# A gated linear recurrence on one Trainium2 core: the diagonal and the first two levels of a chunk as one visit over groups of four tokens

## The chip, the core and the metric

The kernel runs on one core of a Trainium2 chip. The metric is the device time of one execution in microseconds (us), the median of several runs. The engines named below are TensorE (PE; PEld is its weight load), VectorE (DVE), ScalarE (ACT), GpSimd (POOL) and SyncE (SP), which starts the DMAs.

## What is computed

A two-layer model over 1024 tokens and 1024 channels in float32: sliding-window attention and a squared-ReLU MLP, then the HGRN2 recurrence and a second MLP. Only the recurrence is touched. It has 8 heads with 128 key and 128 value channels, and the tokens stand in chunks of 64:

```python
q, f, i, g = jnp.split(h @ w_in, 4, axis=-1)
forget = lb + (1.0 - lb) * jax.nn.sigmoid(f)
k = 1.0 - forget
...
b = jnp.cumsum(lc, axis=2)                    # lc = log(forget), one chunk
o_inter = einsum('bhtd,bhde->bhte', qc * jnp.exp(b), state)
diff = b[:, :, :, None, :] - b[:, :, None, :, :]
decay = jnp.exp(jnp.where(causal, diff, -jnp.inf))
scores = einsum('bhtd,bhtsd,bhsd->bhts', qc, decay, kc)
o_intra = einsum('bhts,bhse->bhte', scores, vc)
...
```

Inside a chunk the score of query t and key s is a sum over the channels of q[t] k[s], times the product of the forget gates of the tokens s+1 to t.

## The kernel before

Channels lie on the partitions and tokens on the free axis, in two halves of 512 tokens (NH = 2). A head has, for each half, tiles of 128 x 512 for q, f (the forget gate), k, v and the output gate g.

**The recurrence of a head** (`recurrence`, lines 1141 to 1229) builds the scores of all 16 chunks without a logarithm or an exponential, by levels. A diagonal visit (lg = -1) multiplies k by q for every chunk (16 matmuls of 64 columns) and keeps the diagonal by a mask; then q is multiplied by f. Level lg = 0 to 5 joins neighbouring groups of H = 2^lg tokens: 16 matmuls of 32 columns give k against the q of the later group of every pair, a predicated copy with the level's mask puts them into the scores, and `double` (line 1231) multiplies q of the later group by the earlier group's product of gates, k of the earlier group by the later group's, and the products of the gates with each other. A last visit joins chunks in pairs (`cross`), and two more pieces, one for each half, make the states and the outputs. The matmuls of a visit are float32 with 64 weight columns, so the two chunks of a pair lie in the two column halves of the array (`rows`, line 1158). A visit takes one PSUM bank of pool q. Each matmul names all q and k tiles as inputs, so that a visit starts as a whole.

**The pieces around it.** `recurrence` is a generator with 10 pieces: the diagonal, six levels, the cross visit and two halves. `interleave` (line 1312) puts those of head e between the 14 pieces of `gates` of head e + 1, at 10 per 14. A piece of `gates` is one product of the projections (`product`, line 567: 12 matmuls of 128 x 512 with three products of high and low parts); `two` (line 1082) makes 7 of them with Strassen's seven products for a pair of the matrices q, g and then f, v. `strassen_weights` (line 573) loads four raw weights and makes four sums in tiles of pool m; `weight_split` writes the high and low parts into pools wh and wl, five tiles each.

**The order of the work.** Every operation is first recorded (`Schedule.add`, line 150) with its engine, a cost and its tiles; `order` (line 184) then plans the whole kernel as a list schedule. On each engine the ready operation with the lowest rank goes next; the rank is the place in the program, less a lead of 100 for weights and for what empties a bank of pool p. Tiles of a pool are handed out in program order as they come free (BUFS, line 41). The costs are the code's own: 70 + 1.04 n ns for a product or a predicated copy on VectorE, and a drain of 120 ns when TensorE changes between matmuls of the whole array and of column halves. What comes out is a fixed order for each engine; on the chip each engine works its queue in that order and waits by semaphores.

Pools m (7 tiles) and t (18) hold tiles of 512 float32 numbers per partition. m serves the weight sums, the totals and states of the recurrence, attention's scores with their sinks, and the scaled sums of the MLP. t serves nearly everything else that is short-lived.

Of the kernel before, what the change touches and what calls it, by code (L numbers as in the profile page):

```python
# [10 lines left out]
F32 = mybir.dt.float32  # L11
F32R = mybir.dt.float32r
I32 = mybir.dt.int32
AF = mybir.ActivationFunctionType
ALU = mybir.AluOpType
AX = mybir.AxisListType

P = 128
# [3 lines left out]
NH = 2  # L22
# [17 lines left out]
PI_DOWN = float(np.float32(3.1415925))  # L40
BUFS = {"a": 60, "t": 18, "m": 7, "sm": 8, "wr": 5, "wh": 5, "wl": 5, "p": 4, "q": 4}
CH = 64
# [236 lines left out]
class Net:  # L279
# [490 lines left out]
    def rope_tables(self):  # L770
        shape = (P, NBLK, ROT // 2)
        pos = self.const((P, NBLK), I32)
        self.dma(pos, self.io["pos"], 4 * P * NBLK)
        posf = self.const((P, NBLK))
        self.op("DVE", self.nc.vector.tensor_copy, [posf], [pos], 100, posf, pos)
        ang = self.const(shape)
        for j, f in enumerate(INV_FREQ):
            self.ts("DVE", ang[:, :, j], posf, f, None, ALU.mult, None, NBLK)
        self.trig = []
        for shift in (0.25, 0.0):  # L780
            turns, r = self.const(shape), self.const(shape)
            n = NBLK * ROT // 2
            self.ts("DVE", turns, ang, float(0.5 / np.pi), shift, ALU.mult, ALU.add, n)
            self.ts("DVE", turns, turns, MAGIC, MAGIC, ALU.add, ALU.subtract, n)
            self.stt(r, turns, -TWO_PI[0], ang, ALU.mult, ALU.add, n)
            self.stt(r, turns, -TWO_PI[1], r, ALU.mult, ALU.add, n)
            self.stt(r, turns, -TWO_PI[2], r, ALU.mult, ALU.add, n)
            if shift:
                self.ts("DVE", r, r, float(np.pi / 2), None, ALU.add, None, n)
            self.ts("DVE", r, r, PI_DOWN, -PI_DOWN, ALU.min, ALU.max, n)  # L790
            self.act(r, r, AF.Sin, n)
            self.trig.append(r)
# [233 lines left out]
    def hgrn_constants(self):  # L1026
# [23 lines left out]
        self.level_mask = []  # L1050
        for lg in range(LEVELS):
            mask, later = self.const((P, CH), I32), self.t(I32, (P, CH))
# [4 lines left out]
            self.tt("DVE", mask, mask, later, ALU.mult, CH)  # L1057
            self.level_mask.append(mask)

    def put_by(self, views):  # L1060
# [80 lines left out]
    def recurrence(self, e, gates, totals, out):  # L1141
# [4 lines left out]
        scores = self.t(F32, (P, NC, CH))  # L1146
        tots, tot = [self.t(tag="m") for _ in range(NH)], [g[1] for g in gates]
        at = 0
        for lg in range(-1, LEVELS):
            H = 1 << max(lg, 0)  # L1150
            n, width = (1, CH) if lg < 0 else (CH // (2 * H), CH // 2)
            part = self.psum("q")[:, : NC * width].rearrange("p (c t) -> p c t", c=NC)
            later = lambda z: z if lg < 0 else z.rearrange("p (n a h) -> p n a h", a=2, h=H)[:, :, 1]
            both = [z for q, f, k, g, v in gates for z in (q, k)]
            for hf, (q, f, k, g, v) in enumerate(gates):
                for c in range(BPH):
                    for b in range(2):
                        rows = slice(b * CH, b * CH + CH)
                        j = 2 * c + b
                        self.mm(part[rows, hf * BPH + c], chunk(k, j), later(chunk(q, j)), True, True, CH, 2.06, "columns", both)  # L1160
            if lg < 0:
                mask = self.diag.unsqueeze(1).to_broadcast([P, NC, CH])
                self.tt("DVE", scores, part, mask, ALU.mult)
                for q, f, k, g, v in gates:
                    self.tt("any", q, q, f, ALU.mult)
                yield
                continue
            mask = later(self.level_mask[lg]).unsqueeze(1).to_broadcast([P, NC, n, H])
            target = scores.rearrange("p c (n a h) -> p c n a h", a=2, h=H)[:, :, :, 1]
# [21 lines left out]
        for hf, (q, f, k, g, v) in enumerate(gates):  # L1191
# [36 lines left out]
            out[hf].append(self.put_by(y) if keep else y)  # L1228
            yield

    def double(self, H, gates, tot, tots, at):

# [164 lines left out]
```

## Time and profile before

| | before |
|---|---|
| median of 3 runs | 2162.72 us (2162.41 to 2163.83) |
| profiled execution, its own time | 2167.06 us |
| its span | 2165.3 us |
| granted TensorE clock, mean | 0.995 |
| TensorE matmul busy | 2130.3 us (98%), 11464 instructions |
| weight load busy | 1721.6 us (80%) |
| VectorE busy | 1801.3 us (83%), 3531 instructions |
| ScalarE busy | 855.2 us (39%) |
| GpSimd busy | 60.5 us (3%) |
| float32 matmuls of 64 weight columns and 32 columns (levels) | 1536 instructions, 54.0 us busy |
| the same with 64 columns (diagonal, cross) | 384 instructions, 18.6 us busy |
| predicated copies of the levels, VectorE | 48, 25.8 us busy |

The profile is that of one execution. Its span goes from the first to the last instruction; the execution's own time holds a little more. In its lines L333 is the line of the helper that records every operation, so the tiles tell operations apart: out<-in by pool name, then the weight size, the shapes and a count. A float32 matmul stands as two instructions. A matmul's end is modelled, so the distance from start to start says more than the duration. "idle before <-releaser" is time in which the engine waited, and for what.

### The profile page before, as it was taken

The numbers are of one execution on the slowest core, as the hardware profiler recorded it, in microseconds if no ns is written. First come the engines' busy times: TensorE is split into PE (matmuls) and PEld (weight loads), VectorE is DVE, ScalarE is ACT, GpSimd is POOL, SyncE is SP. The second block draws the span as 40 slices with busy tenths as digits, with TensorE's granted clock in tenths as the row PEclk, the third lists the DMA queues.
The fourth block names the chain that finished last, engine by engine and source line by source line (L and its number), as shares of the span: only waits on it lengthen the run. The fifth ranks groups of instructions, "written<-read, shape, count | busy, mean of one in ns | idle before, by whom it ended". The sixth has DMA issues, their size and how long they took to land.

```text
span 2165.3 us, 32388 instructions
## 1 busy us (share of the span) xinstructions
PE 2130.3 (98%) x11464; PEld 1721.6 (80%) x11464; DVE 1801.3 (83%) x3531; ACT 855.2 (39%) x1791; POOL 60.5 (3%) x121
## 2 busy tenths in 40 slices
PE   9999999999999999999999999999999999999998
PEld 7778777888887887877788888888788887888887
DVE  8889889666789888899888888878877678988886
ACT  5567764212234233365333333343421223423444
POOL 4020000000000000000100000000000000000000
PEclk9999999999999999999999999999999999999999
DMA  6212273333368867741111111547333336976652
GB/s 210 79 49 83 79 241 99 112 107 107 111 219 298 261 208 230 249 135 54 59 55 59 55 59 59 186 156 228 101 109 107 103 117 218 301 254 211 216 180 78
DMA packets 174274, 316.50 MB, mean 146 GB/s; under 512 B 19616, under 2 KB 21664, under 8 KB 174112
## 3 DMA queue, kind: packets, MB, share of 16 engines
q1 hardware_dynamic: 174112, 314.43, 45.1%
q8 instruction: 90, 1.47, 0.3%
q14 instruction: 72, 0.59, 0.1%
HBM read 250.39 MB, written 63.96 MB: 145 GB/s over the span
## 4 chain that ended last, share of the span: by engine, by line
PE 54%; issue 36%; DVE 5%; ACT 3%; DMA 2%; SPq 0%; POOL 0%; POOLq 0%; ACTq 0%; DVEq 0%
PE p L333 28%; PE q L333 26%; DVE a L333 2%; DVE t L333 1%; ACT a L333 1%; ACT t L333 1%; DVE wl L333 1%; DVE m L333 1%; DMA a<-d 1%; DMA wr<-in_down 0%; ACT wh L333 0%; DMA wr<-in_wqkv 0%; DMA a<-in_x 0%; DVE sm L333 0%; DVE wh L333 0%
## 5 line engine op out<-in xcount | busy, mean ns | idle before, releaser
L333 PE MATMUL q<-a,wh 128*128 128x512 f32 x2560 | 799.7, 395 | 8.7 <-DVE t L333 3.7
L333 PE MATMUL p<-a,wh 128*128 128x512 f32 x2336 | 752.7, 401 | 4.1 <-ACT wh L333 3.3
L333 PEld LDWEIGHTS q<-a,wh 128*128 128x128 f32 x2560 | 480.9, 188 | 123.1 <-ACT t L333 5.2
L333 PEld LDWEIGHTS p<-a,wh 128*128 128x128 f32 x2336 | 431.7, 189 | 100.1 <-ACT wh L333 4.2
L333 PE MATMUL q<-a,wl 128*128 128x512 f32 x1280 | 500.1, 394 | 0.2 <-DVE wl L333 0.2
L333 PE MATMUL p<-a,wl 128*128 128x512 f32 x1168 | 462.5, 397 | 1.8 <-DVE wl L333 1.7
L333 PEld LDWEIGHTS q<-a,wl 128*128 128x128 f32 x1280 | 240.8, 188 | 57.5 <-DVE wl L333 0.6
L333 PEld LDWEIGHTS p<-a,wl 128*128 128x128 f32 x1168 | 220.3, 189 | 51.9 <-DVE wl L333 2.7
L333 DVE TENSOR_TENSOR wl<-wr,wh 128x512 fp32r<-128x512 f32 x352 | 240.6, 685 | 15.2 <-ACT wh L333 6.2
L333 ACT COPY t<-q 128x512 f32<-128x512 f32 (+2 forms) x201 | 111.7, 562 | 356.8 <-PE q L333 348.6
L333 DVE TENSOR_TENSOR a<-t,a 128x512 fp32r<-128x512 f32 (+1 forms) x294 | 194.3, 682 | 2.3 <-DMA t<-d 2.0
L333 DVE TENSOR_TENSOR wl<-m,wh 128x512 fp32r<-128x512 f32 x256 | 176.0, 688 | 16.5 <-ACT wh L333 7.3
L333 ACT CAST wh<-m 128x512 fp32r<-128x512 f32 x155 | 96.6, 623 | 219.5 <-PE q L333 151.2
L333 DVE CAST wh<-wr 128x512 fp32r<-128x512 f32 x189 | 80.7, 427 | 117.3 <-PE p L333 71.7
L333 DVE TENSOR_TENSOR t<-t,t 128x512 f32<-128x512 f32 (+3 forms) x265 | 157.0, 610 | 18.3 <-DMA t<-d 13.4
L333 ACT CAST a<-t 128x512 fp32r<-128x512 f32 x195 | 118.2, 619 | 127.3 <-PE q L333 82.5
L333 ACT CAST wh<-wr 128x512 fp32r<-128x512 f32 x163 | 100.6, 620 | 167.5 <-PE p L333 100.3
L333 DVE TENSOR_TENSOR m<-wr,wr 128x512 f32<-128x512 f32 x160 | 109.4, 686 | 27.3 <-DMA wr<-in_up 12.9
L333 PE MATMUL p<-wh,a 128*128 128x512 f32 x384 | 126.3, 399 | 0.4 <-ACT a L333 0.2
L333 PEld LDWEIGHTS q<-t,t 128*64 128x64 f32 (+1 forms) x2160 | 98.0, 144 | 25.1 <-PE p L333 10.9
L333 PE MATMUL q<-t,t 128*64 128x32 f32 (+2 forms) x2160 | 111.5, 230 | 0.0
L333 DVE CAST wh<-m 128x512 fp32r<-128x512 f32 x101 | 43.4, 429 | 75.3 <-PE q L333 61.8
(118 smaller groups left out, 2113.1 us busy)
## 6 DMA issues: line engine op xcount, KB each, us to landing
t<-d SPq DMA_DIRECT2D x296, 256.0 KB, 4.7
wr<-in_down SPq DMA_DIRECT2D x256, 256.0 KB, 4.0
d<-t SPq DMA_DIRECT2D x180, 256.0 KB, 2.6
wr<-in_up SPq DMA_DIRECT2D x128, 256.0 KB, 3.0
wr<-in_win SPq DMA_DIRECT2D x68, 256.0 KB, 2.9
a<-d SPq DMA_DIRECT2D x60, 256.0 KB, 4.4
wr<-in_wqkv SPq DMA_DIRECT2D x48, 256.0 KB, 3.0
d<-a SPq DMA_DIRECT2D x48, 256.0 KB, 3.4
```

The lines of the kernel that those rows point to most:

```text
L333: fn(*[place(a) for a in args], **{k: place(v) for k, v in kw.items()})
```

## The change

The diagonal and the levels lg = 0 and 1 become one piece, `fours`, over groups of four tokens. Before the matmuls, VectorE makes for each half a tile w with six more columns of queries for each group of four (the queries of tokens 1, 2 and 3 multiplied by the gates that lie between them and the keys of the same group). 16 matmuls of 64 columns then give k against q, and 16 of 96 columns k against w; they take three banks of pool q. One masked product and six predicated copies put the results into the scores. Fourteen more products bring q, k and the totals to where `double` left them after lg = 1. The levels lg = 2 to 5 stay. `recurrence` has 8 pieces instead of 10; `interleave` is called with the same numbers.

Pool t goes from 18 tiles to 17 and pool m from 7 to 6; the angle and turn tables of the rotary embedding, three constants before, are taken from pool t. The masks of the first two levels go, and three masks for the groups of four come.

```diff
@@ -38,7 +38,7 @@
 MAGIC = 12582912.0
 TWO_PI = (6.28125, 2029.0 / 2**20, 2 * np.pi - 6.28125 - 2029.0 / 2**20)
 PI_DOWN = float(np.float32(3.1415925))
-BUFS = {"a": 60, "t": 18, "m": 7, "sm": 8, "wr": 5, "wh": 5, "wl": 5, "p": 4, "q": 4}
+BUFS = {"a": 60, "t": 17, "m": 6, "sm": 8, "wr": 5, "wh": 5, "wl": 5, "p": 4, "q": 4}
 CH = 64
 LEVELS = 6
 K_SPANS = ((-1, 3), (2, 6), (5, 8))
@@ -769,16 +769,17 @@
 
     def rope_tables(self):
         shape = (P, NBLK, ROT // 2)
+        flat = lambda: self.t()[:, : NBLK * ROT // 2].rearrange("p (n d) -> p n d", n=NBLK)
         pos = self.const((P, NBLK), I32)
         self.dma(pos, self.io["pos"], 4 * P * NBLK)
         posf = self.const((P, NBLK))
         self.op("DVE", self.nc.vector.tensor_copy, [posf], [pos], 100, posf, pos)
-        ang = self.const(shape)
+        ang = flat()
         for j, f in enumerate(INV_FREQ):
             self.ts("DVE", ang[:, :, j], posf, f, None, ALU.mult, None, NBLK)
         self.trig = []
         for shift in (0.25, 0.0):
-            turns, r = self.const(shape), self.const(shape)
+            turns, r = flat(), self.const(shape)
             n = NBLK * ROT // 2
             self.ts("DVE", turns, ang, float(0.5 / np.pi), shift, ALU.mult, ALU.add, n)
             self.ts("DVE", turns, turns, MAGIC, MAGIC, ALU.add, ALU.subtract, n)
@@ -1048,7 +1049,7 @@
         self.diag = self.const((P, CH))
         self.ts("DVE", self.diag, bits, 0, None, ALU.is_equal, None, CH)
         self.level_mask = []
-        for lg in range(LEVELS):
+        for lg in range(2, LEVELS):
             mask, later = self.const((P, CH), I32), self.t(I32, (P, CH))
             self.ts("DVE", mask, bits, lg, None, ALU.logical_shift_right, None, CH)
             self.ts("DVE", mask, mask, 1, None, ALU.is_equal, None, CH)
@@ -1056,6 +1057,17 @@
             self.ts("DVE", later, later, 0, None, ALU.is_gt, None, CH)
             self.tt("DVE", mask, mask, later, ALU.mult, CH)
             self.level_mask.append(mask)
+        same, s4, d4 = (self.t(I32, (P, CH)) for _ in range(3))
+        self.ts("DVE", same, bits, 2, None, ALU.logical_shift_right, None, CH)
+        self.ts("DVE", same, same, 0, None, ALU.is_equal, None, CH)
+        self.ts("DVE", s4, si, 3, None, ALU.bitwise_and, None, CH)
+        self.tt("DVE", d4, ti, si, ALU.subtract, CH)
+        self.four_mask = []
+        for z, value in ((s4, 0), (d4, 1), (s4, 1)):
+            mask = self.const((P, CH), I32)
+            self.ts("DVE", mask, z, value, None, ALU.is_equal, None, CH)
+            self.tt("DVE", mask, mask, same, ALU.mult, CH)
+            self.four_mask.append(mask)
 
     def put_by(self, views):
 
@@ -1144,13 +1156,13 @@
         NC = NH * BPH
         chunk = lambda z, j: z[:, j * CH : j * CH + CH]
         scores = self.t(F32, (P, NC, CH))
-        tots, tot = [self.t(tag="m") for _ in range(NH)], [g[1] for g in gates]
-        at = 0
-        for lg in range(-1, LEVELS):
-            H = 1 << max(lg, 0)
-            n, width = (1, CH) if lg < 0 else (CH // (2 * H), CH // 2)
+        tots = [self.t(tag="m") for _ in range(NH)]
+        at, tot = yield from self.fours(gates, scores, tots)
+        for lg in range(2, LEVELS):
+            H = 1 << lg
+            n, width = CH // (2 * H), CH // 2
             part = self.psum("q")[:, : NC * width].rearrange("p (c t) -> p c t", c=NC)
-            later = lambda z: z if lg < 0 else z.rearrange("p (n a h) -> p n a h", a=2, h=H)[:, :, 1]
+            later = lambda z: z.rearrange("p (n a h) -> p n a h", a=2, h=H)[:, :, 1]
             both = [z for q, f, k, g, v in gates for z in (q, k)]
             for hf, (q, f, k, g, v) in enumerate(gates):
                 for c in range(BPH):
@@ -1158,14 +1170,7 @@
                         rows = slice(b * CH, b * CH + CH)
                         j = 2 * c + b
                         self.mm(part[rows, hf * BPH + c], chunk(k, j), later(chunk(q, j)), True, True, CH, 2.06, "columns", both)
-            if lg < 0:
-                mask = self.diag.unsqueeze(1).to_broadcast([P, NC, CH])
-                self.tt("DVE", scores, part, mask, ALU.mult)
-                for q, f, k, g, v in gates:
-                    self.tt("any", q, q, f, ALU.mult)
-                yield
-                continue
-            mask = later(self.level_mask[lg]).unsqueeze(1).to_broadcast([P, NC, n, H])
+            mask = later(self.level_mask[lg - 2]).unsqueeze(1).to_broadcast([P, NC, n, H])
             target = scores.rearrange("p c (n a h) -> p c n a h", a=2, h=H)[:, :, :, 1]
             part = part.rearrange("p c (n h) -> p c n h", n=n)
             self.op("DVE", nc.vector.copy_predicated, [target], [mask, part], 70 + NC * width * 1.04, target, mask, part)
@@ -1228,6 +1233,63 @@
             out[hf].append(self.put_by(y) if keep else y)
             yield
 
+    def fours(self, gates, scores, tots):
+        nc, NC, W = self.nc, NH * BPH, 6 * CH // 4
+        chunk = lambda z, j: z[:, j * CH : j * CH + CH]
+        N, new, more = TH // 4, [], []
+        for hf, (q, f, k, g, v) in enumerate(gates):
+            w = self.tile("w", 2, (P, 6 * N), F32)
+            qv, fv = (z.rearrange("p (n b) -> p n b", b=4) for z in (q, f))
+            wv = w.rearrange("p (n c) -> p n c", c=6)
+            mul = lambda out, x, y, n: self.tt("DVE", out, x, y, ALU.mult, n * N)
+            mul(wv[:, :, 0:1], qv[:, :, 1:2], fv[:, :, 1:2], 1)
+            mul(wv[:, :, 1:4:2], qv[:, :, 2:4], fv[:, :, 2:4], 2)
+            mul(wv[:, :, 2:6:3], wv[:, :, 1:4:2], fv[:, :, 1:3], 2)
+            mul(wv[:, :, 4:5], wv[:, :, 5:6], fv[:, :, 1:2], 1)
+            more.append(w)
+        diag = self.psum("q").rearrange("p (c t) -> p c t", c=NC)
+        six = [self.psum("q")[:, : BPH * W].rearrange("p (c t) -> p c t", c=BPH) for _ in range(NH)]
+        both = [z for q, f, k, g, v in gates for z in (q, k)] + more
+        for hf, (q, f, k, g, v) in enumerate(gates):
+            for c in range(BPH):
+                for b in range(2):
+                    rows, j = slice(b * CH, b * CH + CH), 2 * c + b
+                    self.mm(diag[rows, hf * BPH + c], chunk(k, j), chunk(q, j), True, True, CH, 2.06, "columns", both)
+        for hf, (q, f, k, g, v) in enumerate(gates):
+            for c in range(BPH):
+                for b in range(2):
+                    rows, j = slice(b * CH, b * CH + CH), 2 * c + b
+                    self.mm(six[hf][rows, c], chunk(k, j), more[hf][:, j * W : j * W + W], True, True, W, 2.0, "columns", both)
+        self.tt("DVE", scores, diag, self.diag.unsqueeze(1).to_broadcast([P, NC, CH]), ALU.mult)
+        for hf in range(NH):
+            part = six[hf].rearrange("p c (n k) -> p c n k", k=6)
+            target = scores[:, hf * BPH : hf * BPH + BPH].rearrange("p c (n b) -> p c n b", b=4)
+            for mask, t, src, m in zip(self.four_mask, (1, 2, 3), (slice(0, 5, 2), slice(1, 4, 2), slice(5, 6)), (3, 2, 1)):
+                mask = mask.rearrange("p (n b) -> p n b", b=4)[:, :, t:].unsqueeze(1).to_broadcast([P, BPH, CH // 4, m])
+                out, in_ = target[:, :, :, t:], part[:, :, :, src]
+                self.op("DVE", nc.vector.copy_predicated, [out], [mask, in_], 70 + BPH * CH // 4 * m * 1.04, out, mask, in_)
+        for hf, (q, f, k, g, v) in enumerate(gates):
+            qv, fv, kv = (z.rearrange("p (n b) -> p n b", b=4) for z in (q, f, k))
+            wv = more[hf].rearrange("p (n c) -> p n c", c=6)
+            mul = lambda out, x, y, n: self.tt("DVE", out, x, y, ALU.mult, n * N)
+            first = fv[:, :, 0:1]
+            mul(qv[:, :, 0:1], qv[:, :, 0:1], first, 1)
+            mul(qv[:, :, 1:4], wv[:, :, 0:5:2], first.to_broadcast([P, N, 3]), 3)
+            mul(kv[:, :, 2:3], kv[:, :, 2:3], fv[:, :, 3:4], 1)
+            tail = self.t()[:, : 2 * N].rearrange("p (n b) -> p n b", b=2)
+            mul(tail[:, :, 1:2], fv[:, :, 2:3], fv[:, :, 3:4], 1)
+            mul(tail[:, :, 0:1], fv[:, :, 1:2], tail[:, :, 1:2], 1)
+            mul(kv[:, :, 0:2], kv[:, :, 0:2], tail, 2)
+            new.append(tots[hf][:, :N].only(4))
+            mul(new[hf].unsqueeze(2), first, tail[:, :, 0:1], 1)
+        yield
+        return N, new
     def double(self, H, gates, tot, tots, at):
 
         n, new = TH // (2 * H), []
```

## Prediction

> **What bounds the kernel now.** I read the busy time by stage first, then TensorE's waits inside the recurrence stage, then single visits in order of time. Columns of the first view: stretch, its length, busy time (and instructions) of TensorE matmul, weight load, VectorE, ScalarE, GpSimd, then granted clock, DMA share, GB/s.
>
> ```profile
> 85.00:292.00 207.00, 202.61 (x1191) 158.35 (x1190) 183.64 (x407) 148.88 (x480) 21.39 (x49) 1.00 0.28 85
> 292.00:1003.00 711.00, 701.86 (x3030) 565.86 (x3031) 585.72 (x1033) 258.01 (x455) 0.37 (x2) 1.00 0.55 177
> 1003.00:1440.00 437.00, 434.98 (x3692) 352.80 (x3691) 377.43 (x866) 155.86 (x327) 9.68 (x18) 1.00 0.24 77
> 1440.00:2166.00 726.00, 710.29 (x3195) 580.33 (x3194) 583.39 (x1023) 245.44 (x442) 3.87 (x3) 0.99 0.54 173
> ```
>
> The recurrence runs from 1003 to 1440 us. TensorE is idle there for 437.00 - 434.98 = 2.0 us in all; VectorE is busy 377.43 / 437 = 86%, ScalarE 36%. TensorE's matmul ends are modelled, so I also ask what it waits for in that stage:
>
> ```profile
> PE q L333 <- DVE m L333: 1.0, 2, 0.6
> PE q L333 <- ACT t L333: 0.7, 2, 0.4
> PE q L333 <- DVE a L333: 0.4, 1, 0.4
> ```
>
> Five waits, 2.1 us. So in this stage a microsecond taken off TensorE's queue is a microsecond off the end, and work on another engine costs nothing until TensorE has to wait for it. The place of the change, in the middle of one head (start, duration, operation, count):
>
> ```profile
> 1182.83 0.39 PE L333 MATMUL p<-a,wl 128*128 128x512 f32 x1
> 1183.15 1.15 PE L333 MATMUL q<-t,t 128*64 128x64 f32 x32
> 1184.23 0.74 PE L333 MATMUL p<-a,wh 128*128 128x512 f32 x2
> ...
> 1185.04 0.62 PE L333 MATMUL p<-a,wh 128*128 128x512 f32 x2
> ...
> 1185.74 0.63 PE L333 MATMUL p<-a,wh 128*128 128x512 f32 x2
> ...
> 1186.90 0.40 PE L333 MATMUL p<-a,wl 128*128 128x512 f32 x1
> 1187.22 1.12 PE L333 MATMUL q<-t,t 128*64 128x32 f32 x32
> 1188.28 0.72 PE L333 MATMUL p<-a,wh 128*128 128x512 f32 x2
> ```
>
> The projections (p<-a) of the next head run without a break; between them stand the visits (q<-t,t). Three projection matmuls take 1185.74 - 1185.04 = 0.70 us, 0.23 each. The diagonal visit (64 columns, 16 matmuls shown as 32 instructions) pushes the next projection from 1182.83 to 1184.23: 1.40 us, less the 0.23 that the matmul before it takes, is **1.17 us**. The first level's visit (32 columns) pushes from 1186.90 to 1188.28: 1.38 - 0.23 = **1.15 us**. Half the columns cost the same. The instructions come in pairs, one for each column half of the array. What one takes by itself:
>
> ```profile
> L333 PE MATMUL q<-t,t x2160: 222/223/377, 1017.4 to 1438.1; 128*64 128x32 f32 x140, 128*64 128x64 f32 x34, 128*128 128x128 f32 x23
> L333 PE MATMUL q<-t,a x368: 276/379/430, 85.9 to 290.7; 128*64 128x256 f32 x120, 128*128 128x256 f32 x64
> ```
>
> The last one's modelled 0.22 us (the median of the first row, in ns) aside, 16 pairs start within 1.12 - 0.22 = 0.90 us at 32 columns and 0.93 at 64: 0.06 us a pair, whatever the width. The rest of each visit, 1.17 - 0.93 = 0.24 us, is the change of form before and after.
>
> **What goes and what comes on TensorE.** Per head, a 64-column and two 32-column visits go: 1.17 + 1.15 + 1.15 = 3.47 us. A 64-column set and, behind it in the same form, a 96-column set come. No instruction of 96 columns is in the trace. One side is the 64-column row: 0.06 us a pair. The other is the 256-column row of attention, in the same form:
>
> ```profile
> 143.97 3.24 PE L333 MATMUL q<-t,a 128*64 128x256 f32 x28
> 147.14 0.33 PE L333 MATMUL q<-c,a 128*128 128x128 f32 x1
> ```
>
> 28 instructions are 14 pairs; one takes 0.38 (the row above), so 13 steps take 3.24 - 0.38 = 2.86 us, 0.22 a pair. Between 0.06 at 64 and 0.22 at 256 columns a straight line gives 0.06 + 0.16 x 32/192 = 0.087 us at 96. I take that, since the width governs at 256 and the 64-column set sits where it just begins to. Then 16 x 0.087 = 1.39 us, and the new visit costs 1.17 + 1.39 = 2.56 us. Saved: 3.47 - 2.56 = **0.91 us a head, 7.3 us over eight heads**. At 0.06 a pair it would be 16 x 0.06 = 0.96 us, saved 1.34 a head, 10.7 in all. Should the planner put projections between the two sets, one more change of form (0.24) comes back: 0.67 a head, 5.4 in all.
>
> A rule speaks against the line. The Trainium skill (TensorE: Matmul & The Clock Gate, Part 3, "The mechanism") says that a weight load overlaps matmuls in flight only where their row groups differ; here both halves use all 128 rows. By that rule load and stream would add up, which is the second rival below; the trace does not bear it out, since 256 columns at 0.22 us a pair leave no room for a load on top.
>
> **What comes on VectorE.** Steps between starts (shown durations overlap by about 0.08):
>
> ```profile
> 1143.60 0.43 DVE L333 COPY_PREDICATED t<-c,q 128x256 f32<-128x256 int32 x1
> 1143.93 1.42 DVE L333 TENSOR_TENSOR t<-t,m 128x256 f32<-128x256 f32 x4
> 1145.27 0.68 DVE L333 SCALAR_TENSOR_TENSOR t<-t,t 128x512 f32<-128x512 f32 x1
> ...
> 1185.43 1.29 DVE L333 TENSOR_TENSOR t<-t,t 128x512 f32<-128x512 f32 x2
> 1186.63 0.69 DVE L333 TENSOR_TENSOR m<-wr,m 128x512 f32<-128x512 f32 x1
> ...
> 1188.84 0.73 DVE L333 COPY_PREDICATED t<-c,q 128x256 f32<-128x256 int32 x1
> 1189.37 1.46 DVE L333 TENSOR_TENSOR t<-t,t 128x256 f32<-128x256 f32 x4
> 1191.13 0.43 DVE L333 CAST wh<-wr 128x512 fp32r<-128x512 f32 x1 [0.31 <-PE p L333]
> ```
>
> A product of 512 takes (1186.63 - 1185.43)/2 = 0.60 us, of 256 (1145.27 - 1143.93)/4 = 0.335; that is 0.07 + 0.00104 n, so 0.20 at 128 and 0.47 at 384. A predicated copy of 256 takes 0.53 at the first level (1188.84 to 1189.37) and 0.33 at the third (1143.60 to 1143.93): short runs are slow, 0.07 + 0.0018 n. The new copies have runs of one to three elements, so I take the slow price.
> - Before, a head: diagonal mask 0.60, q by f twice 0.60, first level 0.53 + 4 x 0.345 + two totals of 256 at 0.335, second level 0.53 + 4 x 0.345 + two totals of 128 at 0.20: 6.7 us in 17 instructions.
> - After: the six columns, (128 + 256 + 256 + 128) a half, 1.08, twice: 2.2; mask 0.60; copies of 192, 128 and 64 a half, 0.42 + 0.30 + 0.19, twice: 1.8 (fast price: 1.2); then five products of 128, one of 384, one of 256 a half, 1.82, twice: 3.6. Sum 8.2 us in 29 instructions.
>
> That is 1.5 us more a head, 12 us in all; VectorE goes from 377 of 437 us to about 389 of 430, 91%. TensorE hides it as long as the next visit is not late, which is the one new wait. From the new visit to the third level's visit VectorE has copies and 14 products to do, about 5.5 us instead of the 2 of a level. In-order TensorE meets that visit where the planner put it; what is queued behind it is the next head's projections, and everything on TensorE waits with them. The planner's costs in the code (70 + 1.04 n ns) give the six copies 1.22 us, I 1.8: a slip of 0.58. What a slip does is seen in the last head, where the visits come as soon as they can:
>
> ```profile
> 1410.09 1.47 DVE L333 TENSOR_TENSOR t<-t,t 128x256 f32<-128x256 f32 x4
> 1411.47 0.69 DVE L333 TENSOR_TENSOR wl<-wr,wh 128x512 fp32r<-128x512 f32 x1
> ```
> ```profile
> 1411.38 0.39 PE L333 MATMUL p<-a,wh 128*128 128x512 f32 x1
> 1411.70 1.12 PE L333 MATMUL q<-t,t 128*64 128x32 f32 x32
> ```
>
> There copy and products took 0.53 + 1.38 = 1.91 us against 1.68 planned, and the visit still followed its forerunner after 0.32 us, as at 1182.83 and 1186.90. A slip of 0.23 is swallowed; of 0.58 at most 0.35 shows, less what VectorE's own pauses (0.31 us at 1191.13) take up. I put **0.2 us a head, 1.6 us** on TensorE, with 0 and 0.35 as ends. The 2.2 us for the six columns delay the new visit, and projections fill the time.
>
> **Edits priced at nothing.** The setup keeps 30 mask operations of 64 columns. The rope tables keep theirs and only change buffers. The new visit holds three q banks instead of one; the products use p banks, and ScalarE, which empties the transposes' banks ahead, is idle 64% of the stage. The recurrence now has 8 pieces, still spread at 10 per 14 steps, so its last pieces and their stores to DRAM go through SP's queue earlier in each head; the DMA share is 0.24, and none of TensorE's five waits is for a DMA. Pool m goes from 7 to 6. In attention GpSimd writes the sinks ahead into every m tile that comes free:
>
> ```profile
> L333 ACT COPY m<-q x6: 348/370/375, 86.3 to 95.5; 128x256 f32<-128x256 f32 x6
> L333 PE MATMUL q<-c,m x4: 272/273/300, 95.4 to 95.8; 128*128 128x128 f32 x4
> L333 POOL TENSOR_SCALAR m<-c x1: 226/226/226, 96.2 to 96.2; 128x4 f32<-128x4 f32 x1
> ```
>
> When it refills the first freed tile (96.2) only three blocks (six copies) have begun, one of them ended: seven tiles were taken, three at work. Six are enough. For t, 18 to 17, no view counts the live tiles. TensorE's waits in the other stages are 4.4, 9.1 and 15.7 us (first view); a tenth of them, 3 us, bounds what a new order of the same work does there, either way. I take 0.
>
> **Sum.** The profiled execution took 2167.06 us, 1.8 more than its span and 4.3 more than the median of the three runs. 2167.06 - 7.3 + 1.6 = 2161.4; the same -5.7 from the median 2162.72 is **2157.0 us**. A measurement tells about 0.2% from no change, 4.3 us.
>
> **Rivals.**
> 1. *VectorE's longer chain shows in full (0.18).* If the slip of 0.58 and 0.15 more from strided products (14 of them, 0.01 each by the first level's 0.345 against 0.335) all land on TensorE at the third level's visit, 8 x 0.73 = 5.8 us come back: -7.3 + 5.8 gives 2161.2, no change. For it: VectorE at 91%. Against: TensorE's waits on VectorE in this stage are 1.4 us today.
> 2. *Loads add to the stream at 96 columns (0.06).* The 0.06 a pair at 32 columns would be a load floor, and a 96-column pair would take 0.06 + 0.087: 16 x 0.147 = 2.35 us instead of 1.39, 7.7 us more in all: -5.7 + 7.7 = +2.0, 2164.7. Against: the 256-column row, and 32 and 64 columns costing alike.
> 3. *Slower: the weights' sums run out of m tiles (0.09).* The rows:
>
> ```profile
> 1170.86 1.11 DVE L333 SCALAR_TENSOR_TENSOR m<-m,m,q 128x128 f32<-128x128 f32 x3 [0.91 <-ACT m L333]
> ...
> 1177.72 0.34 DVE L333 SCALAR_TENSOR_TENSOR m<-m,m,q 128x128 f32<-128x128 f32 x1
> 1177.98 0.68 DVE L333 TENSOR_TENSOR m<-wr,wr 128x512 f32<-128x512 f32 x1
> ...
> 1183.53 0.69 DVE L333 TENSOR_TENSOR wl<-m,wh 128x512 fp32r<-128x512 f32 x1
> ```
>
> Each set of projections sums its weights in four m tiles; two totals and up to two state tiles hold four more (1170.86 to 1177.98), and the next set's first sum does start right behind the last state. With six tiles it may start one tile's life, up to 7 us, later. Five weight buffers of one product (12 matmuls, 2.8 us) each are ahead, so it decides only once about 11 us are used up. Two microseconds beyond that in each head are 16 us: 2157.0 + 16 = 2173. Against: no wait on wl is among TensorE's five.
>
> The forecast has 0.60; 0.07 is left for an order of the other stages that gives or takes more than 3 us. **Range:** low 2151.5, the 0.06 price (-10.7) with no wait, 2152.0, and a little of the other stages; high 2164.7, the second rival. **Chances:** faster by over 0.2%: 0.61 (nearly all of the forecast and half the 0.07), the same: 0.28, slower: 0.11.
>
> **What would show it.** In the profile after: a 64- and a 96-column set back to back, the second some 1.4 us long (0.087 a pair), and six visits a head where there were eight; VectorE 12 us busier in the stage; the third level's visit following its projection after more than 0.32 us in most heads if the first rival holds; waits for wl if the third. I am wrong if the stage from the first to the last visit is not 4 to 9 us shorter, or if another stage moves by more than 3.

## The result, and the profile after

The kernel after took **2176.40 us** (median of 6 runs, 2174.40 to 2178.09), the kernel before beside it 2162.56 (6 runs, 2162.24 to 2165.05). The ratio is 1.0062, 95% interval 1.0049 to 1.0074: slower by 13.8 us, where 5.7 us less had been forecast. The profiled execution took 2177.95 us, span 2176.2.

The stages of the kernel after from 292 us on, in the columns of the first view of the prediction:

```profile
292.00:1003.00 711.00, 701.55 (x3023) 565.63 (x3024) 584.00 (x1028) 256.68 (x452) 0.36 (x2) 0.99 0.53 177
1003.00:1440.00 437.00, 426.21 (x3419) 346.58 (x3418) 388.56 (x927) 167.79 (x356) 8.17 (x18) 1.00 0.23 76
1440.00:2176.00 736.00, 718.10 (x3217) 586.07 (x3217) 586.43 (x1028) 248.18 (x447) 3.85 (x3) 0.99 0.52 171
```

In the recurrence VectorE is busy 11 us more, about the forecast 12. But TensorE, idle for 2.0 us there before, now has 437.00 - 426.21 = 10.8 us of idle time. What it waits for between 1010 and 1445 us (in total, times, longest):

```profile
PE q L333 <- DVE t L333: 6.0, 7, 1.1
PE q L333 <- ACT t L333: 4.3, 6, 0.8
PE q L333 <- DVE a L333: 0.4, 1, 0.4
```

Seven waits for VectorE and six for ScalarE: nearly one of each in every head. TensorE in order of time, in one head of the middle:

```profile
1184.40 0.66 PE L333 MATMUL q<-c,t 128*128 128x128 f32 x4 [0.71 <-ACT t L333]
...
1186.29 0.39 PE L333 MATMUL p<-a,wl 128*128 128x512 f32 x1
1186.61 1.15 PE L333 MATMUL q<-t,t 128*64 128x64 f32 x32
1187.59 1.49 PE L333 MATMUL q<-w,t 128*64 128x96 f32 x32
1189.01 0.73 PE L333 MATMUL p<-a,wh 128*128 128x512 f32 x2
...
1193.29 0.63 PE L333 MATMUL p<-a,wh 128*128 128x512 f32 x2
1193.84 0.66 PE L333 MATMUL q<-t,t 128*64 128x32 f32 x16
1195.27 0.66 PE L333 MATMUL q<-t,t 128*64 128x32 f32 x16 [0.77 <-DVE t L333]
1195.86 0.50 PE L333 MATMUL p<-a,wl 128*128 128x512 f32 x1
```

The new visit is as forecast: two sets back to back. They push the next projection from 1186.29 to 1189.01, 2.72 us. Less the 0.23 of the matmul before them that is **2.49 us** (forecast 2.56). TensorE stops twice in this head. The third level's visit falls into two halves of 16 instructions, and the second waits 0.77 us for VectorE. Earlier in the head the transposes at 1184.40 wait 0.71 us for ScalarE. What VectorE does ahead of each (start, duration, operation):

```profile
1179.14 0.41 DVE L333 TENSOR_TENSOR w<-t,t 128x128 f32<-128x128 f32 x1
1179.44 0.39 DVE L333 TENSOR_TENSOR t<-t 128x128 f32<-128x128 f32 x1
1179.74 0.51 DVE L333 TENSOR_TENSOR w<-t,t 128x256 f32<-128x256 f32 x1
1180.12 0.38 DVE L333 TENSOR_TENSOR t<-t,t 128x128 f32<-128x128 f32 x1
1180.41 0.50 DVE L333 TENSOR_TENSOR w<-w,t 128x256 f32<-128x256 f32 x1
...
1182.01 0.69 DVE L333 TENSOR_TENSOR t<-t,a 128x512 f32<-128x512 f32 x1
...
1190.15 0.45 DVE L333 COPY_PREDICATED t<-c,q 128x192 f32<-128x192 int32 x1
...
1194.21 0.67 DVE L333 TENSOR_TENSOR wl<-wr,wh 128x512 fp32r<-128x512 f32 x1
1194.81 0.41 DVE L333 TENSOR_TENSOR t<-t,t 128x256 f32<-128x256 f32 x1
```
```profile
1182.73 0.63 ACT L333 ACTIVATE t<-t 128x512 f32<-128x512 f32 x1 [2.35 <-DVE t L333]
```

From start to start a product of 128 elements takes 1179.44 - 1179.14 = 0.30 us. The plan's cost and the prediction's were 0.20. The row product at 1182.01, which ScalarE's step at 1182.73 is waiting for, stands behind five such products. The keys' last product (1194.81), which the third level's second half is waiting for, ends a row of six copies and eight products that begins at 1190.15.

Outside the recurrence the wait that stands out is just ahead of it, TensorE first, then VectorE:

```profile
975.25 1.18 PE L333 MATMUL p<-a,wh 128*128 128x512 f32 x4
982.48 0.79 PE L333 MATMUL p<-a,wl 128*128 128x512 f32 x1 [6.05 <-DVE wl L333]
```
```profile
976.92 2.50 DVE L333 TENSOR_TENSOR t<-t,t 128x512 f32<-128x512 f32 x4
979.33 0.69 DVE L333 TENSOR_TENSOR m<-wr,m 128x512 f32<-128x512 f32 x1
...
981.73 0.69 DVE L333 TENSOR_TENSOR wl<-m,wh 128x512 fp32r<-128x512 f32 x1
```

A weight sum (m<-wr,m) and the low half made from it (wl<-m,wh) stand in VectorE's order behind row products, and the projection waits 6.05 us. The granted clock is low for a while (the last three columns are granted clock, DMA share and GB/s):

```profile
976.00:982.40 6.40, 0.43 (x2) 0.00 (x0) 6.40 (x12) 6.40 (x13) 0.00 (x0) 0.76 0.16 41
982.40:989.30 6.90, 6.82 (x22) 5.46 (x23) 6.90 (x13) 1.40 (x4) 0.00 (x0) 0.72 0.11 38
```

The 6.90 us after the wait run at 0.72: 1.9 us lost on top of the 6.05. The kernel before has its own, shorter stop near there, 46 us earlier:

```profile
936.40 1.81 PE L333 MATMUL p<-a,wh 128*128 128x512 f32 x4 [3.11 <-ACT wh L333]
```
```profile
937.00:941.00 4.00, 4.00 (x12) 3.10 (x12) 4.00 (x12) 2.47 (x5) 0.00 (x0) 0.61 0.00 0
```

So there are two places to test: the recurrence, and the stages around it.

### The profile page after: what moved, and what is told of

Same layout as the page of the kernel before. It is cut to its first block, busy times and chain, and to the rows that moved or that the text cites. A ratio compares the mean times of both kernels' runs of the same rounds, so it can differ in the third digit from the quotient of the medians.

```text
span 2176.2 us, 32039 instructions
## 1 busy us (share of the span) xinstructions
PE 2130.2 (98%) x11208; PEld 1722.7 (79%) x11208; DVE 1816.0 (83%) x3600; ACT 865.4 (40%) x1818; POOL 64.6 (3%) x121
## 4 chain that ended last, share of the span: by engine, by line
PE 47%; issue 37%; DVE 11%; ACT 3%; DMA 2%; POOL 0%; SPq 0%; POOLq 0%; DVEq 0%; ACTq 0%
PE q L333 26%; PE p L333 22%; DVE t L333 5%; DVE a L333 2%; DVE wl L333 2%; ACT a L333 1%; DVE m L333 1%; ACT t L333 1%; DVE w L333 1%; DMA t<-d 1%; ACT wh L333 0%; DMA wr<-in_down 0%; DMA a<-in_x 0%; DVE wh L333 0%; DMA wr<-in_up 0%
## 5 line engine op out<-in xcount | busy, mean ns | idle before, releaser
L333 ACT CAST wh<-m 128x512 fp32r<-128x512 f32 x172 | 106.7, 621 | 237.1 <-PE q L333 152.1
L333 DVE TENSOR_TENSOR t<-t,t 128x512 f32<-128x512 f32 (+4 forms) x282 | 163.1, 587 | 16.7 <-DMA t<-d 14.2
L333 ACT CAST a<-a 128x512 fp32r<-128x512 f32 x106 | 65.1, 622 | 111.8 <-PE q L333 55.9
L333 PEld LDWEIGHTS q<-t,t 128*64 128x64 f32 (+1 forms) x1648 | 82.3, 145 | 27.4 <-DVE t L333 8.6
L333 PE MATMUL q<-t,t 128*64 128x32 f32 (+2 forms) x1648 | 94.7, 232 | 6.1 <-DVE t L333 6.0
```

Source lines behind the costliest of these rows:

```text
L333: fn(*[place(a) for a in args], **{k: place(v) for k, v in kw.items()})
```

## A yardstick for both places

A stage's length misleads here, because the planner moves projections across its edges: between the first and the last visit stand 1215 projection matmuls before and 1223 after. The middle heads are comparable: between one 64-column visit and the next stand 168 such matmuls on average over the four heads taken here, in every kernel below. Four heads, from the third head's visit to the seventh's, last (1350.70 - 1127.28)/4 = 55.86 us before:

```profile
1127.28 1.15 PE L333 MATMUL q<-t,t 128*64 128x64 f32 x32
...
1350.70 1.15 PE L333 MATMUL q<-t,t 128*64 128x64 f32 x32
```

and 56.50 after:

```profile
1130.10 1.15 PE L333 MATMUL q<-t,t 128*64 128x64 f32 x32
...
1356.09 1.15 PE L333 MATMUL q<-t,t 128*64 128x64 f32 x32
```

Eight times the difference to before is taken as what the recurrence gives or takes; the rest of the change in the median is "elsewhere". The first and last heads differ from the middle ones, the heads come from one execution and the medians from five to twelve. The intervals of the ratios alone are 2 to 5 us wide to each side, so "elsewhere" is no better than that. The ratio is the recorded one; it is not that of the two medians and differs from it by up to 0.0011. All kernels (t and m: the two pools; difference of the median to that of before on the same chip, which was 2162.56, 2163.68, 2164.48 and 2164.19 us in the four sets):

| kernel | t, m | difference, us | ratio, 95% interval | a middle head, us | times 8, us | elsewhere, us |
|---|---|---|---|---|---|---|
| after | 17, 6 | +13.8 | 1.0049 to 1.0074 | 56.50 | +5.1 | +8.7 |
| before, both pools smaller | 17, 6 | +10.7 | 1.0032 to 1.0075 | 56.22 | +2.9 | +7.8 |
| before, m smaller | 18, 6 | +1.6 | 0.9992 to 1.0013 | 56.02 | +1.3 | +0.3 |
| before, t smaller | 17, 7 | +6.1 | 1.0014 to 1.0039 | 56.29 | +3.5 | +2.6 |
| before, t larger | 19, 6 | +6.9 | 1.0018 to 1.0039 | 55.89 | +0.2 | +6.7 |
| before, another order | 18, 7 | +3.2 | 1.0005 to 1.0022 | 55.85 | 0.0 | +3.2 |
| after, contiguous products | 17, 6 | +1.3 | 0.9983 to 1.0008 | 55.14 | -5.7 | +7.0 |
| after, measured costs | 17, 6 | +0.5 | 0.9990 to 1.0015 | 55.13 | -5.8 | +6.3 |
| the same, wr 5 | 18, 5 | -3.2 | 0.9966 to 0.9989 | 54.68 | -9.4 | +6.3 |
| the same, wr 4 | 18, 6 | -4.0 | 0.9969 to 0.9996 | 54.65 | -9.6 | +5.6 |
| the same, wh 4, wl 4 | 18, 7 | +4.1 | 1.0008 to 1.0029 | 55.10 | -6.0 | +10.1 |
| the same, wr 4 | 19, 5 | +5.8 | 1.0019 to 1.0036 | 54.94 | -7.3 | +13.1 |
| after, planned costs, wr 5 | 18, 5 | +2.1 | 0.9996 to 1.0013 | 56.03 | +1.4 | +0.7 |

## Experiments: the pools by themselves

The kernel before with the two pools of the kernel after, and nothing else of the change:

```
-BUFS = {"a": 60, "t": 18, "m": 7, ...
+BUFS = {"a": 60, "t": 17, "m": 6, ...
```

> The kernel before with nothing but pool t at 17 and pool m at 6. Theory A (the recurrence comes out even, because its own waits eat the saved visits, and the 11 us of longer span come from the other stages, whose order the smaller pools change): 8 to 12 us slower than before, 2170 to 2175, with a wait of several us for wl near 975 us. Rival B (the other stages get longer because of what the changed recurrence leaves behind in the plan, and the pools cost nothing): within 2 us of before.

Measured: 2174.34 us against 2163.68. Most of the loss, 10.7 of 13.8 us (7 to 16 by the interval), comes without any new visit. The wait ahead of the recurrence comes with it:

```profile
980.98 0.80 PE L333 MATMUL p<-a,wl 128*128 128x512 f32 x1 [6.74 <-DVE wl L333]
```

All four kernels with 17 t and 6 m tiles show this wait (6.05 to 6.74 us), whatever their recurrence. It is not theirs alone: three of the later variants with other pools stop for 5.8 to 6.9 us between 980 and 990 us. One pool at a time, m 6 first, then t 17:

```
-BUFS = {"a": 60, "t": 18, "m": 7, ...
+BUFS = {"a": 60, "t": 18, "m": 6, ...
```

> The kernel before with pool m at 6 alone. Theory A with m as the scarce pool (the weight sums and scaled sums of the MLP's last pass wait for tiles): most of the loss, 5 to 10 us slower than before. If t is the scarce one: within 2 us. Rival B: within 2 us.

```
-BUFS = {"a": 60, "t": 18, "m": 7, ...
+BUFS = {"a": 60, "t": 17, "m": 7, ...
```

> The kernel before with pool t at 17 alone. Theory A with m as the scarce pool: 0 to 3 us slower. With t as the scarce one: 5 to 10 us slower. Rival B: within 2 us.

Measured: 2165.25 (no difference) and 2169.73 (+6.1). The m tile by itself costs nothing, the t tile does, and the two together cost more than their sum. It looked like a shortage of t. The next two runs were made to tell that from the mere order.

## Experiments: shortage or order

One t tile more than before, paid with the m tile that had cost nothing:

```
-BUFS = {"a": 60, "t": 18, "m": 7, ...
+BUFS = {"a": 60, "t": 19, "m": 6, ...
```

> The kernel before, with 19 t tiles and 6 m tiles in place of 18 and 7 (the m tile alone cost nothing). Theory A (the time outside the recurrence falls with the number of t tiles: 17 cost 6 us against 18): 19 is faster by 1 to 4 us. Theory B (17 was slow by the order that the planner fell into, not by a shortage): a change of either sign, within 8 us.

Measured: 2171.13, slower by 6.9 us, with more t than before. The stop before the recurrence is 5.05 us long here, and for another weight half:

```profile
938.75 2.93 PE L333 MATMUL p<-a,wh 128*128 128x512 f32 x6 [5.05 <-ACT wh L333]
```

And the kernel before with its pools, one figure of the planner changed by 10 ns:

```
-    "ACT": {"SP": 200.0, "PE": 260.0, ...
+    "ACT": {"SP": 200.0, "PE": 250.0, ...
```

> The kernel before, with one figure of the planner changed by 10 ns: a result of ScalarE is taken to reach TensorE 250 instead of 260 ns after its step. Pools, instructions and computation are as before; the plan's order differs in many places (some copies change their engine). Theory A (a shortage of t tiles, not the order, cost the 6 to 11 us): within 3 us of before. Theory B (any new order moves the stages around the recurrence by several us): 4 to 10 us of either sign, with waits of TensorE for wl, wh or t at the seams in other places.

Measured: 2167.34, slower by 3.2 us (1.0005 to 1.0022), with the middle head at 55.85, the same as before. That lies between the two expectations. A shortage of t does not explain the first run, which is slower with more t. A new pool size is a new plan, and in the profiles TensorE's long stops around the recurrence stand elsewhere or last longer than in before, with one exception: m 6 alone, which loses nothing either. In the last column of the table all thirteen other kernels (twelve plans, since contiguous products keep the plan of after) lie above before, by 0.3 to 13.1 us; the smallest of these are within the noise. No run shows how the plan of before was come by: had it been picked as the fastest of many, others would lie above it for that reason alone.

Inside the heads a shortage of t is not excluded. In five pairs of the table that differ by 17 against 18 t tiles, alone or with m or wr, the head with 18 is shorter, by 0.2 to 0.5 us: 1.6 to 3.8 us over eight heads. The variant with four wh and wl tiles does not show it.

## Experiments: the visits and VectorE's costs

The kernel after, with the planner told the durations that its profile shows for the new products and copies (and no other change):

```
-mul = lambda out, x, y, n: self.tt("DVE", out, x, y, ALU.mult, n * N)
+mul = lambda out, x, y, n: self.op("DVE", nc.vector.tensor_tensor, [out], [x, y], {1: 305, 2: 390}[n], ...)
...
-    self.op("DVE", nc.vector.copy_predicated, [out], [mask, in_], 70 + BPH * CH // 4 * m * 1.04, ...)
+    self.op("DVE", nc.vector.copy_predicated, [out], [mask, in_], {1: 172, 2: 230, 3: 301}[m], ...)
...
-mul = lambda out, x, y, n: self.tt("DVE", out, x, y, ALU.mult, n * N)
+mul = lambda out, x, y, n: self.op("DVE", nc.vector.tensor_tensor, [out], [x, y], {1: 295, 2: 325, 3: 542}[n], ...)
```

> The changed kernel, with the planner's costs of the new products and copies set to the steps that its own trace shows (295 to 305 ns for 128 strided elements instead of 203, 325 to 390 for 256, 542 for 384; 172, 230 and 301 for the copies). The work is the same, only the order changes. Theory A (TensorE waits at the third level's visit and at the transposes of v because the plan has VectorE too fast): the 0.9 us wait of each head goes, the recurrence gets 5 to 8 us shorter, 2168 to 2172 in all. Rival C (the waits come from ScalarE or from what the semaphores cost, not from the planned costs): the same as the changed kernel, 2175 to 2178.

Measured: 2164.13 us, equal to before (+0.5 us) where the kernel after stands at +13.8. VectorE does nearly the same work (473 instructions in the four heads instead of 478) at the same durations, but TensorE no longer meets the third level's visit too early. Its waits from 1010 to 1445 us:

```profile
PE q L333 <- ACT t L333: 1.9, 6, 0.4
PE p L333 <- DVE t L333: 0.9, 1, 0.9
PE q L333 <- DVE a L333: 0.4, 1, 0.4
PE q L333 <- DVE sm L333: 0.3, 1, 0.3
```

3.5 us instead of 10.7, and the third level's visit is one set again, with a projection right ahead of it:

```profile
1188.58 0.40 PE L333 MATMUL p<-a,wh 128*128 128x512 f32 x1
1188.90 1.12 PE L333 MATMUL q<-t,t 128*64 128x32 f32 x32
1189.96 0.50 PE L333 MATMUL p<-a,wh 128*128 128x512 f32 x1
```

The planned costs are not the only thing that differs there: another plan is another order. So the reverse was run: the plan of the kernel after kept, and VectorE made as fast as that plan believes. Each product takes contiguous columns of the same number instead of every fourth one (the weighted queries and keys then hold other values):

```
-mul(wv[:, :, 0:1], qv[:, :, 1:2], fv[:, :, 1:2], 1)
+mul(w[:, :N], q[:, N : 2 * N], f[:, N : 2 * N], 1)
...
-mul(kv[:, :, 0:2], kv[:, :, 0:2], tail, 2)
+mul(k[:, : 2 * N], k[:, : 2 * N], tail[:, : 2 * N], 2)
```

> The kernel after, with every product of the groups of four taken on contiguous columns of the same number instead of on every fourth one (so its weighted queries and keys hold other values; the instructions, their number and their order are the same, and so are the planned costs). Theory A (the products with a 16-byte stride cost the extra VectorE time: 0.29 to 0.31 us for 128 elements where the plan has 0.20): the 128-element products start 0.20 us apart, VectorE is about 1 us a head shorter, TensorE's 0.9 us stand in the third level's visit and the 0.7 us before the transposes shrink to under 0.5 us together, and the time falls by 6 to 9 us, to about 2169. Theory B (the products wait for one another's results, or the copies are the late ones): the same steps as after, 0.3 us, and 2176 within 2.

Measured: 2165.74, +1.3 us to before instead of +13.8, with the same instructions in the same order on every engine. That is more than the 6 to 9 us expected; 10.8 us of it are the recurrence's. The same products on VectorE:

```profile
1182.14 0.28 DVE L333 TENSOR_TENSOR t<-t,t 128x128 f32<-128x128 f32 x1
1182.33 0.45 DVE L333 COPY_PREDICATED t<-c,q 128x128 f32<-128x128 int32 x1
...
1185.39 0.27 DVE L333 TENSOR_TENSOR t<-t,t 128x128 f32<-128x128 f32 x1
1185.58 0.69 DVE L333 TENSOR_TENSOR wl<-wr,wh 128x512 fp32r<-128x512 f32 x1
```

0.19 us from start to start, where the strided ones take 0.29 to 0.31. And TensorE, in the same head:

```profile
1123.90 1.15 PE L333 MATMUL q<-t,t 128*64 128x64 f32 x32
...
1185.76 0.63 PE L333 MATMUL p<-a,wh 128*128 128x512 f32 x2
1186.32 1.13 PE L333 MATMUL q<-t,t 128*64 128x32 f32 x32
1187.37 0.50 PE L333 MATMUL p<-a,wl 128*128 128x512 f32 x1
...
1344.47 1.15 PE L333 MATMUL q<-t,t 128*64 128x64 f32 x32
```

The two halves of the visit now run without a break, and four heads take (1344.47 - 1123.90)/4 = 55.14 us each against 56.50. The two experiments meet from both sides: slow products with a plan that knows it, and fast products with the plan that believed it, give the same head within 0.02 us. So the 1.36 us a head (10.8 us over eight) are the distance between a product's planned and its real duration, not VectorE's load.

## Experiments: the pools given back

The kernel after with the pools of before and all else as it is was not run. These variants pay for the t tile elsewhere; each is the kernel with the measured costs and one line changed. First m 5:

```
-BUFS = {"a": 60, "t": 17, "m": 6, ...
+BUFS = {"a": 60, "t": 18, "m": 5, ...
```

> The kernel after with the measured VectorE costs in the plan, and its pools set to 18 t tiles and 5 m tiles in place of 17 and 6. Theory A (the loss of the t tile costs 6 us and more, an m tile nothing, as the two kernels before with one pool changed say): 2164.1 less 6 to 10, 2154 to 2158, less than before by 5 to 8. Theory B (the pools act through the order that the planner falls into, not through a shortage of t): anything, 2160 to 2172; and with five m tiles the attention and the weight sums may wait for m, seen as wl waits at the projections: 2168 to 2175.

Then wr 4:

```
-BUFS = {"a": 60, "t": 17, "m": 6, "sm": 8, "wr": 5, ...
+BUFS = {"a": 60, "t": 18, "m": 6, "sm": 8, "wr": 4, ...
```

> As the run before, but 18 t, 6 m and 4 instead of 5 wr tiles. Theory A: 2154 to 2158. Theory B (order, or the raw weights now come too late, seen as wr loads waiting for their tiles and wl waits at the projections): 2162 to 2175.

Measured: 2161.30 and 2160.46 against 2164.48. Both are faster than before (0.9978, interval 0.9966 to 0.9989, and 0.9982, 0.9969 to 0.9996) and by 17 us or more than after, though less than was expected: the gain of the t tile is in the head (54.65 us, half a microsecond less than with 17), and elsewhere they stay at about +6. These are the versions that beat both kernels. Then 18 and 7, paid with the weight halves:

```
-BUFS = {"a": 60, "t": 17, "m": 6, "sm": 8, "wr": 5, "wh": 5, "wl": 5, ...
+BUFS = {"a": 60, "t": 18, "m": 7, "sm": 8, "wr": 5, "wh": 4, "wl": 4, ...
```

> As the run before, but 18 t and 7 m tiles as in the kernel before, paid with one wh and one wl tile (4 each). Theory A: 2154 to 2158 if four pairs of weight halves are enough for the projections, whose columns are split half a column ahead of their use. Theory B (the halves are made too late): a wait for wl or wh at many projections, 0.1 us at each of the 30 columns of blocks or more: 2165 to 2180.

Measured: 2168.57. The halves do not run out at each column of blocks, since the head is 55.10; the loss is ahead of the recurrence, where two stops stand out. The first is there in before too (3.11 us), the second is not:

```profile
937.89 2.50 PE L333 MATMUL p<-a,wh 128*128 128x512 f32 x5 [3.38 <-ACT wh L333]
...
989.29 0.80 PE L333 MATMUL p<-a,wl 128*128 128x512 f32 x1 [6.80 <-DVE wl L333]
```

Then 19 t tiles, with 5 m and 4 wr:

```
-BUFS = {"a": 60, "t": 17, "m": 6, "sm": 8, "wr": 5, ...
+BUFS = {"a": 60, "t": 19, "m": 5, "sm": 8, "wr": 4, ...
```

> The kernel after with the measured VectorE costs and 19 t, 5 m and 4 wr tiles. Theory A: 1 to 3 us faster than with 18 t tiles, 2157 to 2160. Theory B: anywhere from 2155 to 2168.

Measured: 2169.97; more t, and slower by 9 us than with 18, though m or wr is smaller too. This is the same answer as in the kernel before. Last, the kernel after with its planned costs as they are, and 18 t and 5 m tiles:

```
-BUFS = {"a": 60, "t": 17, "m": 6, ...
+BUFS = {"a": 60, "t": 18, "m": 5, ...
```

> The kernel after, planned costs as they are, with 18 t and 5 m tiles in place of 17 and 6. Theory A (shortage of t): 2176.4 less 3 (what the tile gave beside the measured costs) to less 10 (what the two pools cost in the kernel before), 2166 to 2173. Theory B (order): either sign, 2168 to 2182. In both the recurrence stays where it is in after, its third level's visit split and 0.9 us late in each head.

Measured: 2166.28, +2.1 us to before. The third level's visit is still split, and its second half waits in the middle head for

```profile
1190.75 0.66 PE L333 MATMUL q<-t,t 128*64 128x32 f32 x16
1191.93 0.66 PE L333 MATMUL q<-t,t 128*64 128x32 f32 x16 [0.52 <-DVE t L333]
```

0.52 us instead of 0.77; the head is 56.03 and the recurrence still costs 1.4 us. Elsewhere it is within 1 us of before: this plan has no stop over 3.2 us ahead of the recurrence. So the two losses come and go separately. This variant takes away the one elsewhere, and the slip in the heads is still there: with the same pools and the measured costs a head takes 54.68, again 1.36 us less (before rounding). The measured costs by themselves do the reverse.

## Why the prediction was wrong

**TensorE's saving was right.** The 96-column set lasts 1.49 us; less the 0.25 of its last instruction it is 1.24 over 15 steps, 0.083 us a pair against 0.087. The whole visit costs 2.49 us against 2.56, so 3.47 - 2.49 = 0.98 us a head are saved against 0.91. With the stall at the third level gone the head is shorter by 0.72 (contiguous products) and 0.73 (measured costs), because TensorE still waits 0.3 us a head there for the transposes. That this is the forecast's -0.91 + 0.2 = -0.71 is luck: the forecast's 0.2 was a wait at another place. Where these heads hold no wait at all (18 t, wr 4) the head is 1.20 shorter. The second rival, load and stream added up, would have made a pair 0.147 and falls; by the Trainium skill's rule (TensorE: Matmul & The Clock Gate, Part 3, "The mechanism") the two would not overlap here, and the 0.083 speaks against it. The same section also lets a load into the background weight buffer run ahead of matmuls in flight, and the 0.083 would agree with that.

**The step "I put 0.2 us a head, 1.6 us on TensorE" failed.** Its mechanism, an in-order visit that comes before VectorE is done, was right; its size is 1.36 us a head, seven times as much, and beyond the end of 0.35 and the first rival's 0.73. The head was to be 0.71 shorter and is 0.64 longer. The slip was sought in the copies, and it lies in the products:
- The copies take 1.41 us a head, as three of 0.301, 0.230 and 0.172 us a half. The prediction had 1.8 for runs of one to three elements, the plan 1.22.
- The products on every fourth element take 0.29 to 0.31 us for 128 elements instead of 0.20; the products into the six columns 0.38 to 0.40 for 256, instead of 0.335. The product of 384, three neighbours of every four, takes 0.54 instead of 0.47, but that is not the stride: with contiguous columns it takes 0.53. Together the six columns are 2.8 us a head (forecast 2.2) and the later products 4.7 (3.6). The first rival allowed 0.01 each for the stride, from the first level's rows. Those read every second element; no row that the prediction read had every fourth.
- With the mask's 0.60 that is 9.5 us a head instead of 8.2. The plan had 7.0 for what took 8.9 without the mask: 1.9 us of slip, of which 1.36 showed. The stride makes 1.5 of the 1.9: with contiguous products VectorE is busy 196.36/4 = 49.1 us a head instead of 202.31/4 = 50.6. The slip shows at two places. In the row from 1190.15 on, four products of 128 are 0.09 us late each, two of 384 by 0.07 each and the six copies by 0.19 together: 0.69 us, beside the wait of 0.77. And of the six columns the prediction said that projections fill the time, but the transposes ahead of the new visit hang on the same VectorE queue (the 0.71 us).

One page bears on this. The Trainium skill (SBUF — State Buffer, Specifications (TRN2)) says that SBUF has cachelines of 16 bytes, that full bandwidth needs two or more hits in a line, and that each cross to a new line costs. Every fourth fp32 element is one use a line, every second two; the 0.30 against 0.20 us and the first level's 0.345 against 0.335 agree with that, and so does the product of 384, whose operands use a line two or three times.

**The step "I take 0" for the pools failed,** and with it "a tenth of them, 3 us, bounds what a new order does there". In the kernel after the stages elsewhere cost 8.7 us, with the same pools and the old recurrence 7.8. The count of m tiles in attention was right as far as it went (the m tile alone costs nothing), and the question was the wrong one: not whether the tiles suffice, but that another count makes another plan. Twelve other plans cost 0.3 to 13.1 us elsewhere, and one stop of 6 us is twice the bound by itself. The third rival saw a wait for weight sums and a loss, and had neither place nor size: the wait comes once, ahead of the recurrence, not in each head.

**The signs named beforehand.** The set of 1.4 us and six visits a head came. VectorE's 12 us came too (11), but by luck: its new work is 9.5 us a head against the old 6.7, 22 us over eight heads, and the planner gave 30 conversions (CAST) of the stage to ScalarE, which is 12 us busier. "The third level's visit following its projection after more than 0.32 us" came in another form: the first half follows at once, the second one waits. "Another stage moves by more than 3" was the sign that the forecast was wrong, and it came. The length from first to last visit was a poor sign: it grew by 2.9 us, 1.9 of them for eight projections that the planner moved in.

**What stays open.** The loss elsewhere has no single place. TensorE's idle time between 292 and 1003 us is 9.4 us after and 9.1 before, so the 6.05 us stop partly replaces others; after 1440 us it is 17.9 against 15.7. Nor does such a stop make a kernel slow by itself: the fastest one (18 t, wr 4) has one of 6.86 us at 981.85. By the two profiled executions the larger part lies behind the recurrence. The first visit starts at 1017.68 instead of 1017.39 us, with 12 projection matmuls (2.8 us) fewer ahead of it; from the last visit to the end it is 744.6 instead of 736.9 us, with 4 (0.9 us) more. But contiguous products, with the same plan as after, take 740.5 us there, so one execution of each does not settle it. Part of it can be the clock: averaged over all runs the granted clock is 0.9932 in after and 0.9955 in the 26 runs of before beside the first experiments, and 0.0023 of 2170 us is 5 us, at most, since some of the low clock falls into TensorE's idle time. Why 17 t with 6 m tiles puts the weight sum behind the row products, and 17 or 6 alone does not, was not found. That the order, and nothing else about the pools, makes the loss elsewhere is argued from the run with another order (+3.2 us) and the runs with more t; no run shows it for after itself.

## What to carry to other kernels

Where the instruction order is planned from costs, a new form of instruction needs its real duration in the plan before its worth can be judged: on an engine that runs in order, some 0.08 us wrong on each of 22 products a head cost more than the visits saved. Read the element stride of every new operand, and look for a row with the same stride before a price is taken by element count. And a change to a pool's size in such a kernel is a new plan for the whole program: run the old code with the new pools first, and allow some microseconds of loss for it, not zero.

## What the runs showed of the hardware

- VectorE's products slow down with the stride: 128 fp32 elements take 0.20 us contiguous and 0.29 to 0.31 at every fourth element (16 bytes), in the same order of instructions. Three neighbours of every four cost no more than contiguous ones (384 elements: 0.54 and 0.53 us). Predicated copies in runs of one to three elements of a group of four are not slow: 0.17, 0.23 and 0.30 us for 64, 128 and 192.
- In two profiles one stop of TensorE is paid twice. After the 6.05 us wait the granted clock is 0.72 over the next 6.9 us, after the 3.11 us wait of before 0.61 over 4.0 us: 1.9 and 1.6 us more.
